# A decoder trunk on one core: inverse root on ScalarE with a Newton step, x for sums on the queue of weights, sum steps tied to value tiles

## The chip, the core and the metric

The kernel runs on one core of one Trainium2 chip. A core has five engines with queues of their own: PE (TensorE, the matrix unit), DVE (VectorE), ACT (ScalarE), POOL (GpSimd) and SP (SyncE, here only an issuer of transfers). Each works through its own instructions in order and waits for the others by semaphores. The metric is the device time of one execution in microseconds (us); before the change three runs took 1052.62, 1054.11 and 1057.05, a median of 1054.11.

## The reference

One layer of a decoder trunk on 512 tokens of width 1024, all in fp32. One projection of x gives queries, keys and values for three attentions and three gates; the branches are projected, gated, summed and projected again; a layer norm follows, then a squared-ReLU MLP with a gated embedding, and a second norm. What the change touches is in these lines:

```python
# differential attention: two softmax maps, and an RMS norm of each head's output
w = prob[:, :, 0] - lam * prob[:, :, 1]
o = o * lax.rsqrt(jnp.mean(jnp.square(o), axis=-1, keepdims=True) + RMS_EPS) * norm_g

# dilated attention, (window, dilation) = (128,1), (512,4), (2048,16); heads of one slot
# are combined by the softmax of their log-denominators
wts = jax.nn.softmax(jnp.stack(lses, axis=0), axis=0)
o = wts[0][..., None] * outs[0] + wts[1][..., None] * outs[1] + wts[2][..., None] * outs[2]

m = mixer(x, ...)
x = layer_norm(DEEPNORM_ALPHA * x + m, ln1_g, ln1_b)
hid = jax.nn.relu(x @ w_up)
c = jnp.square(hid) @ w_down
x = layer_norm(DEEPNORM_ALPHA * x + c + sigmoid(x @ w_ple_gate) * (p @ w_ple), ln2_g, ln2_b)
```

## The kernel before, in words

**Products in two parts.** Every weight chunk of 128x1024 fp32 is loaded into a buffer `raw` (L182, on SP's queue), cast on ACT to a high part `wh` (L212), and the rest `wl = raw - wh` is taken on DVE (L214). The other operand is split likewise, and one product is three matmuls: high by high, low by high, high by low (L87 to L89, and the same three in L420 to L422, L453 to L455, L648 to L650 and others). `raw` is a ring of seven buffers, `wh` and `wl` rings of six, so a load, a cast and a subtraction each wait for the ring's oldest buffer.

**Seven products in place of eight.** Larger products are computed in a scheme of seven block products, which needs sums of blocks. Sums of weights are made in DRAM by transfers that add: `sum_steps` (L958) issues them on POOL's queue, each an adding one (L985) or a plain copy (L987), into `vsum`, `msum`, `gsum`, `usum` and `dsum`; later they are loaded like any other weight. Each sum step depends by hand (the line after L987) on `lows[0]`, the fourth to last L214 issued, which spreads the steps over the main stream. How many are issued after each work item is told by a credit: an item adds its size times its rate (2.5 by default, 1.4 for items of value tiles, 0.5 for those of the sevenfold value scheme), and 0.56 late in the kernel.

**Sums of x for the value product** of the dilated heads are made on DVE. `value_forms` (L343) loads the eight blocks of x^T into `xr` (L347, 256 KB each), forms the sums `fr` (L363, L370, L388) and splits them into `u7`, `u6`, `u4`, `u5` (L237 on ACT, L238 on DVE), which are stored in `vf`. `value_pair` (L395) multiplies them (L420 to L422) and combines the results into the value tiles `dl_v` (L427 to L441). `load_xr` (L324) loads x a second time, for the sums of the mixer's gates (L331). Both sets are issued on POOL's queue, tied to the last L214 (`lows[-1]`).

**The main stream and the heads beside it.** The items (one item is the matmuls into one PSUM bank and its evacuation) stand in a list. Between two items `step` (L1814) advances the attention heads that are active: each head is a generator, and a `yield` is a place at which it lets the main stream go on. So where a `yield` stands decides how many products lie on PE between two steps of a head, and, since each engine is in order, what lies in front of each instruction.

**A dilated head** (`dil_head`, L1661): scores on PE (L1677, L1693), bias and maximum on DVE (L1680, L1701), negated maxima (L1684, L1705), exponentials with row sums on ACT (L1686, L1708), per-row statistics gathered (L1711, L1714) and moved to the other token order by small matmuls (L1718, L1720). Then comes a chain of small DVE operations of 128x8 (L1724 to L1740, with one exponential on ACT, L1735) that gives the combining weights; L1742 and L1746 scale the probabilities by them, L1761 and L1770 transpose these on PE, and L1782, L1787 multiply by the values. In head 0 six extra `yield`s stand ahead of L1761.

**A block of differential attention** (`da_block`, L1589): scores (L131, L132), softmax on DVE and ACT (L1600 to L1614), transposes (L1620), product with the values (L1634), squares with their sum on ACT (L1638). The root of the norm is taken of four values per token, `ss`, in a tile of 128x4: L1643 scales and adds on DVE, L1644 raises to the power -1/2 on POOL, L1645 multiplies by the softmax denominators on DVE. L101 on DVE, in another function, writes the low parts of the queries and keys (`da_klb` among them), whose next user is in the chain of products L648.

**Value tiles** that are not made by the sevenfold scheme (`v_items`, L445) are copied out of PSUM by `cp`, which alternates between ACT and DVE.

Of the kernel before, what the change touches and what calls it, by code (L numbers as in the profile page):

```python
# [13 lines left out]
AF = mybir.ActivationFunctionType  # L14
OP = mybir.AluOpType
# [3 lines left out]
P = 128  # L19
# [36 lines left out]
def trunk(tc, a, out):  # L56
    nc = tc.nc
    es = ExitStack()
    with es:
# [17 lines left out]
        def small(name, n):  # L77
            return one.tile([P, n], F32, name=nm(name), tag=f"sm{n}", bufs=12 if n < 8 else 8)
# [14 lines left out]
        def cp(o, i):  # L93
            flip[0] ^= 1
            if flip[0]:
                nc.scalar.copy(o, i)
            else:
                nc.vector.tensor_copy(o, i)
# [37 lines left out]
        ORDERED, AHEAD = 17, 4  # L136
        loads, chunks, placed = [], [], []
        lows = deque(maxlen=4)
        st = {"dma": 0, "split": 0}

        def load(src, w, own=False):
# [56 lines left out]
        def split_next():  # L198
            c = chunks[st["split"]]
            w, off = c["w"], c.get("off", 0)  # L200
            if c.get("pre"):
                c["pre"]()
            if c.get("dst") is None:
                h = ring.tile([P, 1024], F32R, name=nm("wh"), tag="wh", bufs=RING)
                lo = ring.tile([P, 1024], F32R, name=nm("wl"), tag="wl", bufs=RING)
                parts = [(h[:, :w], lo[:, :w], 0, w)]
                c["h"], c["l"] = parts[0][:2]
            else:
                parts = c["dst"]
            for h, lo, a0, a1 in parts:  # L210
                raw = c["from"]["raw"][:, off + a0:off + a1]
                i = nc.scalar.copy(h, raw)  # L212
                st["cast"] = getattr(i, "ins", i)
                i = nc.vector.tensor_sub(lo, raw, h.bitcast(F32))  # L214
                st["low"] = getattr(i, "ins", i)
                lows.append(st["low"])
            for t in (c["from"], *c.get("also", ())):
                t["uses"] -= 1
            st["split"] += 1
# [10 lines left out]
        items = []  # L230
# [14 lines left out]
        xt = a["xT"]  # L245
# [78 lines left out]
        def load_xr():  # L324

            r = {}
            for h in range(2):
                for th in range(2):
                    for kp in range(2):
                        t = slot("xr")  # L330
                        i = nc.gpsimd.dma_start(t.rearrange("p (k t) -> p k t", k=2),  # L331
                                                xt[:, 4 * h + 2 * kp:4 * h + 2 * kp + 2, 256 * th:256 * th + 256])
                        tc.add_manual_dep(getattr(i, "ins", i), lows[-1].name, mybir.DependencyInfo(
                            mybir.DependencyClass.Sync, mybir.DependencyReason.DATA), reason="not ahead of time")
                        r[h, th, kp] = t
            return [[r[h, th, kp] for kp in range(2)] for h in range(2) for th in range(2)]
# [6 lines left out]
        def value_forms():  # L343

            xr = [slot("xr") for _ in range(8)]
            for k, t in enumerate(xr):
                i = nc.gpsimd.dma_start(t, xt[:, k, :])  # L347
                tc.add_manual_dep(getattr(i, "ins", i), lows[-1].name, mybir.DependencyInfo(
                    mybir.DependencyClass.Sync, mybir.DependencyReason.DATA), reason="not ahead of time")

            def blk(kh, k, th):
                return xr[4 * kh + k].rearrange("p (t c) -> p c t", c=4)[:, 2 * th:2 * th + 2, :]

            def new():
                ts = [slot("fr") for _ in range(2)]
                return ts, [ts[k // 2].rearrange("p (k c t) -> p k c t", k=2, c=2)[:, k % 2] for k in range(4)]

            def parts(p, ts):
                form(vf, p, ts)
                vf[p] = [[(h[:, r * P:r * P + P], lo[:, r * P:r * P + P]) for r in range(2)] for h, lo in vf[p]]  # L360

            def neg_sub(o, i, j):
                nc.vector.scalar_tensor_tensor(o, i, -1.0, j, op0=OP.mult, op1=OP.subtract)  # L363

            for _ in range(WAIT):
                yield
            f7, o7 = new()
            with tc.issue_after(st["low"]):
                for k in range(4):
                    nc.vector.tensor_sub(o7[k], blk(1, k, 1), blk(0, k, 1))  # L370
            parts(7, f7)
            yield
            f6, o6 = new()
            with tc.issue_after(st["low"]):
                for k in range(4):
                    neg_sub(o6[k], o7[k], blk(0, k, 0))
            yield
            parts(6, f6)
            yield
            f4, o4 = new()  # L380
            for k in range(4):
                neg_sub(o4[k], o6[k], blk(1, k, 0))
            yield
            parts(4, f4)
            yield
            f1, o1 = new()
            for k in range(4):
                nc.vector.tensor_sub(o1[k], blk(0, k, 0), blk(0, k, 1))  # L388
            yield
            parts(5, f1)  # L390
            yield
# [53 lines left out]
        def v_items(nv, name, g):  # L445
            cs = [chunk(a["wv"][nv, c].rearrange("p k n -> p (k n)"), 1024) for c in range(4)]
            for tt in range(4):
                def mm(ps, tt=tt):
                    for k in range(8):
                        c = cs[k // 2]  # L450
                        s = slice((k % 2) * 512, (k % 2) * 512 + 512)
                        x1, x2 = xh[k][:, tt * P:tt * P + P], xl[k][:, tt * P:tt * P + P]
                        nc.tensor.matmul(ps, x1, c["h"][:, s], start=k == 0, stop=False)  # L453
                        nc.tensor.matmul(ps, x1, c["l"][:, s], start=False, stop=False)  # L454
                        nc.tensor.matmul(ps, x2, c["h"][:, s], start=False, stop=k == 7)  # L455
                        if k == 3:
                            yield

                def ev(ps, tt=tt):
                    if name == "sb_v":  # L460
                        v = [slot(name, F32R).rearrange("p (h two d) -> p h two d", two=2, d=64) for _ in range(2)]
                        pv = ps.rearrange("p (h d) -> p h d", d=64)
                        for i in range(2):
                            hs = slice(4 * i, 4 * i + 4)
                            nc.scalar.copy(v[i][:, :, 0, :], pv[:, hs, :])
                            nc.vector.tensor_sub(v[i][:, :, 1, :], pv[:, hs, :], v[i][:, :, 0, :].bitcast(F32))
                        V[name, g, tt] = v
                    else:
                        t = slot(name)
                        cp(t, ps)  # L470
                        V[name, g, tt] = t
                item(cs if tt == 3 else [], mm, ev, need=cs)
                items[-1]["rate"] = 1.4

        nt, nv = 2, 0
        order = main_order()
# [18 lines left out]
        last_exp = [None]  # L495
# [187 lines left out]
            item([], mm, ev, size=0.08)  # L683

        last_plain = len(items)
        for it in items:
            it.setdefault("rate", 2.5)
        def first_gate(tt, half):
            g = gate_sig(1, tt, half)
            nc.vector.tensor_mul(merged[tt, half], merged[tt, half], g)  # L690
# [267 lines left out]
        def sum_steps():  # L958
# [24 lines left out]
            def issue(o, i, plus):  # L983
                if plus:
                    i = nc.gpsimd.dma_start(o, i, accum_op=OP.add, max_dma_last_dim=4096)  # L985
                else:
                    i = nc.gpsimd.dma_start(o, i, max_dma_last_dim=4096)  # L987

                tc.add_manual_dep(getattr(i, "ins", i), lows[0].name, mybir.DependencyInfo(
                    mybir.DependencyClass.Sync, mybir.DependencyReason.DATA), reason="spread over the main stream")  # L990

            w = a["wv"].rearrange("g c p k n -> g c p (k n)")
# [596 lines left out]
        def da_block(hd, qb):  # L1589
# [50 lines left out]
            if da_left[hd] == 0:  # L1640
                yield

                nc.vector.tensor_scalar(ss, ss, 1.0 / P, EPS, op0=OP.mult, op1=OP.add)  # L1643
                nc.gpsimd.tensor_tensor(ss, ss, mhalf.to_broadcast([P, 4]), OP.pow)  # L1644
                nc.vector.tensor_mul(ss, ss, da_rr[hd])  # L1645
                yield
                on = slot("on")
                nc.vector.tensor_mul(on.rearrange("p (b d) -> p b d", b=4), po.rearrange("p (b d) -> p b d", b=4),
                                     ss.unsqueeze(2).to_broadcast([P, 4, P]))
# [11 lines left out]
        def dil_head(hd):  # L1661
            while any(("dl_q", 4 * g + hd) not in T or ("dl_k", 4 * g + hd) not in T for g in range(3)):
                yield

            while hd == 1 and ("dl_v", 1, 3) not in V:
                yield
            q = [T["dl_q", 4 * g + hd] for g in range(3)]
            k = [T["dl_k", 4 * g + hd] for g in range(3)]
# [77 lines left out]
                nc.vector.tensor_scalar(o, o, mxx[:, c:c + 1], None, op0=OP.mult)  # L1746
            yield

            for _ in range(6 if hd == 0 else 0):
                yield  # L1750

            src0 = {}
# [89 lines left out]
        for n, it in enumerate(items):  # L1842
# [36 lines left out]
            if 12 <= n < wout_at + 12:  # L1879
                credit += it["size"] * it.get("rate", 1.0)  # L1880
            elif n > ple_at + 6:
                credit += 0.56
            while credit >= 1:
                credit -= 1
                next(sum_steps_, None)
# [139 lines left out]
```

## Time and profile before

| what | us |
|---|---|
| three runs, median (lowest to highest) | 1054.11 (1052.62 to 1057.05) |
| the profiled execution, its own time | 1053.95 |
| its span in the trace | 1052.0 |
| PE busy | 1037.5 |
| DVE busy | 763.5 |
| ACT busy | 582.9 |
| POOL busy | 177.7 |

The span goes from the first to the last instruction of the profiled execution; its own time holds some 2 us more around it. Busy times are sums over the instructions of an engine. A row of the waits names an engine and line, what released it, and then the total, the number and the longest of these waits in us. A row of the windows gives a stretch, its length, the busy time of PE, its weight loads (PEld), DVE, ACT and POOL with instructions in brackets, the granted clock, the share of the transfer engines, and GB/s. A row of the timeline gives start, length, engine, line, operation, result and source, shapes, and in square brackets the idle time ahead of it with what ended it. A row of a line gives the shortest, median and longest duration in ns, then the first and last start in us.

### The profile page before, as it was taken

To read this page: it belongs to the slowest core of one execution; us is meant where nothing else is said; L and a number is where in the kernel's file an instruction comes from. 1 tells how busy PE (TensorE), PEld (TensorE's weight loads), DVE (VectorE), ACT (ScalarE), POOL (GpSimd) and SP (SyncE) were. 2 spreads that over 40 slices of the span, in tenths; PEclk is the share of its full clock that TensorE was granted. 3 is DMA by queue.
4 is the path that set the end of the run, shared out by engine and by line. 5 is a ranking of instruction groups with operands and counts; after the bars stand their busy time and mean duration, and the time that the engine had idled before them with its cause. 6 is when DMAs were issued, how large, how long until landed. Compare 5 with 4: busy or idle time off the path is not lost.

```text
span 1052.0 us, 15035 instructions
## 1 busy us (share of the span) xinstructions
PE 1037.5 (99%) x5474; PEld 883.7 (84%) x5474; DVE 763.5 (73%) x1356; ACT 582.9 (55%) x990; POOL 177.7 (17%) x271
## 2 busy tenths in 40 slices
PE   9999999999999999999999999999999999999997
PEld 6887788888888887888888888888999889889885
DVE  6888667749864746788666664888778877877966
ACT  6666545526444645667554723675666665566651
POOL 0012401320203322211121240111121111111000
PEclk9999999999999999999999999999999999999998
DMA  8348965995847999547998996269999899998512
GB/s 320 112 162 256 216 199 195 312 277 186 275 115 220 305 283 271 182 173 238 280 340 269 309 333 198 87 208 324 332 327 320 285 289 295 313 277 281 190 35 80
DMA packets 72761, 254.32 MB, mean 242 GB/s; under 512 B 8968, under 2 KB 9880, under 8 KB 72688
## 3 DMA queue, kind: packets, MB, share of 16 engines
q0 software_dynamic: 32464, 116.21, 42.2%
q1 hardware_dynamic: 39648, 136.24, 35.6%
q8 instruction: 43, 0.70, 0.3%
q10 hardware_dynamic: 576, 0.92, 0.2%
q14 instruction: 30, 0.25, 0.1%
HBM read 251.21 MB, written 106.98 MB: 340 GB/s over the span
## 4 chain that ended last, share of the span: by engine, by line
PE 84%; DMA 9%; DVE 3%; ACT 2%; issue 1%; POOL 0%; SPq 0%; DVEq 0%; POOLq 0%; ACTq 0%
PE mm L87 8%; PE mm L89 7%; PE mm L88 7%; PE at L1147 4%; PE at L1148 4%; PE at L1149 4%; DMA msum<-in_wgm_dram 4%; PE at L556 3%; PE at L555 3%; PE at L554 3%; PE mm L453 2%; PE mm L455 2%; PE mm L454 2%; DMA gsum<-gsum 2%; PE at L89 1%; PE at L88 1%
## 5 line engine op out<-in xcount | busy, mean ns | idle before, releaser
L214 DVE TENSOR_TENSOR wl<-raw,wh 128x1024 fp32r<-128x1024 f32 x251 | 305.3, 1222 | 126.6 <-ACT wh L212 124.4
L212 ACT CAST wh<-raw 128x1024 fp32r<-128x1024 f32 x251 | 262.7, 1050 | 234.0 <-PE mm L88 127.1
L87 PE MATMUL mm<-xhT,wh 128*128 128x512 f32 x304 | 121.1, 398 | 0.0
L89 PE MATMUL mm<-xhT,wl 128*128 128x512 f32 x304 | 119.0, 391 | 0.0
L88 PE MATMUL mm<-xlT,wh 128*128 128x512 f32 x304 | 118.8, 391 | 0.0
L1147 PE MATMUL at<-wh,hh 128*128 128x512 f32 x188 | 73.7, 392 | 0.0
L1148 PE MATMUL at<-wl,hh 128*128 128x512 f32 x188 | 73.7, 392 | 0.0
L87 PE MATMUL mm<-x1hT,wh 128*128 128x256 f32 x256 | 73.6, 288 | 0.0
L1149 PE MATMUL at<-wh,hl 128*128 128x512 f32 x188 | 73.1, 389 | 0.0
L88 PE MATMUL mm<-x1lT,wh 128*128 128x256 f32 x256 | 72.3, 283 | 0.0
L89 PE MATMUL mm<-x1hT,wl 128*128 128x256 f32 x256 | 71.8, 283 | 0.0
L89 PEld LDWEIGHTS mm<-xhT,wl 128*128 128x128 f32 x304 | 57.1, 188 | 12.3
L87 PEld LDWEIGHTS mm<-xhT,wh 128*128 128x128 f32 x304 | 57.2, 188 | 11.6 <-issue 0.4
L88 PEld LDWEIGHTS mm<-xlT,wh 128*128 128x128 f32 x304 | 57.2, 188 | 10.4
L87 PEld LDWEIGHTS mm<-x1hT,wh 128*128 128x128 f32 x256 | 48.8, 191 | 4.7 <-ACT up L1081 2.8
L88 PEld LDWEIGHTS mm<-x1lT,wh 128*128 128x128 f32 x256 | 48.8, 191 | 1.5
L89 PEld LDWEIGHTS mm<-x1hT,wl 128*128 128x128 f32 x256 | 48.6, 191 | 0.0
L985 POOL DMA_DIRECT2D usum<-in_wu_dram x32 | 27.6, 879 | 107.6 <-DVE wl L214 75.7
L1149 PEld LDWEIGHTS at<-wh,hl 128*128 128x128 f32 x188 | 35.3, 188 | 7.7
L1147 PEld LDWEIGHTS at<-wh,hh 128*128 128x128 f32 x188 | 35.5, 189 | 6.0
L1148 PEld LDWEIGHTS at<-wl,hh 128*128 128x128 f32 x188 | 35.5, 189 | 5.5
L985 POOL DMA_DIRECT2D dsum<-in_wd_dram x28 | 23.5, 848 | 96.5 <-DVE wl L214 74.7
(563 smaller groups left out, 2662.3 us busy)
## 6 DMA issues: line engine op xcount, KB each, us to landing
usum<-in_wu_dram POOLq DMA_DIRECT2D x48, 512.0 KB, 9.7
dsum<-in_wd_dram POOLq DMA_DIRECT2D x42, 512.0 KB, 9.0
raw<-in_wt_dram SPq DMA_DIRECT2D x38, 512.0 KB, 6.5
msum<-in_wgm_dram POOLq DMA_DIRECT2D x36, 512.0 KB, 12.7
raw<-usum SPq DMA_DIRECT2D x32, 512.0 KB, 8.1
raw<-dsum SPq DMA_DIRECT2D x28, 512.0 KB, 7.3
raw<-in_wd_dram SPq DMA_DIRECT2D x25, 512.0 KB, 5.3
raw<-msum SPq DMA_DIRECT2D x24, 512.0 KB, 6.0
```

The costliest lines, as they stand in the source:

```text
L87: nc.tensor.matmul(ps, wh, xh, start=start, stop=False, skip_group_check=True)
L88: nc.tensor.matmul(ps, wh, xl, start=False, stop=False, skip_group_check=True)
L89: nc.tensor.matmul(ps, wl, xh, start=False, stop=stop, skip_group_check=True)
L212: i = nc.scalar.copy(h, raw)
L214: i = nc.vector.tensor_sub(lo, raw, h.bitcast(F32))
L554: nc.tensor.matmul(ps, h[:, q], c["h"][:, n], start=go, stop=False, skip_group_check=True)
L555: nc.tensor.matmul(ps, h[:, q], c["l"][:, n], start=False, stop=False, skip_group_check=True)
L556: nc.tensor.matmul(ps, lo[:, q], c["h"][:, n], start=False, stop=end, skip_group_check=True)
L985: i = nc.gpsimd.dma_start(o, i, accum_op=OP.add, max_dma_last_dim=4096)
L1147: nc.tensor.matmul(ps, h[:, q], c["h"][:, s], start=go, stop=False, skip_group_check=True)
L1148: nc.tensor.matmul(ps, h[:, q], c["l"][:, s], start=False, stop=False, skip_group_check=True)
L1149: nc.tensor.matmul(ps, lo[:, q], c["h"][:, s], start=False, stop=end, skip_group_check=True)
```

## The change

Five things are changed.

1. The power on POOL (L1644) is replaced by a logarithm and an exponential on ACT, y = exp(-0.5 ln(ss)), and one Newton step on DVE, y(1.5 - 0.5 ss y y), in three operations of 128x4. The head's `yield` now stands between ACT's part and DVE's. `last_exp` has the table of the sigmoid loaded behind the last of these exponentials.
2. The loads of x for sums (both `value_forms` and `load_xr`) are issued on SP's queue.
3. The copies of value tiles in `v_items` are all on DVE.
4. A second list `marks` of four entries holds each L214 once and each of these copies twice, and the sum steps depend on `marks[0]` in place of `lows[0]`. Rates: value items 2.5 (1.4 before), other items 2.5 for the first 45 and 1.5 behind them (2.5 for all before), and late in the kernel 0.6 (0.56 before).
5. Dilated head 0 begins only when the last sum of x (`vf[5]`) exists, and its extra `yield`s ahead of L1761 are two (six before).

```diff
@@ -136,6 +136,7 @@
         ORDERED, AHEAD = 17, 4
         loads, chunks, placed = [], [], []
         lows = deque(maxlen=4)
+        marks = deque(maxlen=4)
         st = {"dma": 0, "split": 0}
 
         def load(src, w, own=False):
@@ -214,6 +215,7 @@
                 i = nc.vector.tensor_sub(lo, raw, h.bitcast(F32))
                 st["low"] = getattr(i, "ins", i)
                 lows.append(st["low"])
+                marks.append(st["low"])
             for t in (c["from"], *c.get("also", ())):
                 t["uses"] -= 1
             st["split"] += 1
@@ -328,7 +330,7 @@
                 for th in range(2):
                     for kp in range(2):
                         t = slot("xr")
-                        i = nc.gpsimd.dma_start(t.rearrange("p (k t) -> p k t", k=2),
+                        i = nc.sync.dma_start(t.rearrange("p (k t) -> p k t", k=2),
                                                 xt[:, 4 * h + 2 * kp:4 * h + 2 * kp + 2, 256 * th:256 * th + 256])
                         tc.add_manual_dep(getattr(i, "ins", i), lows[-1].name, mybir.DependencyInfo(
                             mybir.DependencyClass.Sync, mybir.DependencyReason.DATA), reason="not ahead of time")
@@ -344,7 +346,7 @@
 
             xr = [slot("xr") for _ in range(8)]
             for k, t in enumerate(xr):
-                i = nc.gpsimd.dma_start(t, xt[:, k, :])
+                i = nc.sync.dma_start(t, xt[:, k, :])
                 tc.add_manual_dep(getattr(i, "ins", i), lows[-1].name, mybir.DependencyInfo(
                     mybir.DependencyClass.Sync, mybir.DependencyReason.DATA), reason="not ahead of time")
 
@@ -467,10 +469,12 @@
                         V[name, g, tt] = v
                     else:
                         t = slot(name)
-                        cp(t, ps)
+                        i = nc.vector.tensor_copy(t, ps)
+                        marks.append(getattr(i, "ins", i))
+                        marks.append(getattr(i, "ins", i))
                         V[name, g, tt] = t
                 item(cs if tt == 3 else [], mm, ev, need=cs)
-                items[-1]["rate"] = 1.4
+                items[-1]["rate"] = 2.5
 
         nt, nv = 2, 0
         order = main_order()
@@ -683,8 +687,8 @@
             item([], mm, ev, size=0.08)
 
         last_plain = len(items)
-        for it in items:
-            it.setdefault("rate", 2.5)
+        for j, it in enumerate(items):
+            it.setdefault("rate", 2.5 if j < 45 else 1.5)
         def first_gate(tt, half):
             g = gate_sig(1, tt, half)
             nc.vector.tensor_mul(merged[tt, half], merged[tt, half], g)
@@ -986,7 +990,7 @@
                 else:
                     i = nc.gpsimd.dma_start(o, i, max_dma_last_dim=4096)
 
-                tc.add_manual_dep(getattr(i, "ins", i), lows[0].name, mybir.DependencyInfo(
+                tc.add_manual_dep(getattr(i, "ins", i), marks[0].name, mybir.DependencyInfo(
                     mybir.DependencyClass.Sync, mybir.DependencyReason.DATA), reason="spread over the main stream")
 
             w = a["wv"].rearrange("g c p k n -> g c p (k n)")
@@ -1641,9 +1645,15 @@
                 yield
 
                 nc.vector.tensor_scalar(ss, ss, 1.0 / P, EPS, op0=OP.mult, op1=OP.add)
-                nc.gpsimd.tensor_tensor(ss, ss, mhalf.to_broadcast([P, 4]), OP.pow)
+                y = small("ir", 4)
+                nc.scalar.activation(y, ss, AF.Ln)
+                e = nc.scalar.activation(y, y, AF.Exp, scale=-0.5)
+                last_exp[0] = getattr(e, "ins", e)
+                yield
+                nc.vector.scalar_tensor_tensor(ss, ss, -0.5, y, op0=OP.mult, op1=OP.mult)
+                nc.vector.tensor_mul(ss, ss, y)
+                nc.vector.scalar_tensor_tensor(ss, ss, 1.5, y, op0=OP.add, op1=OP.mult)
                 nc.vector.tensor_mul(ss, ss, da_rr[hd])
-                yield
                 on = slot("on")
                 nc.vector.tensor_mul(on.rearrange("p (b d) -> p b d", b=4), po.rearrange("p (b d) -> p b d", b=4),
                                      ss.unsqueeze(2).to_broadcast([P, 4, P]))
@@ -1663,6 +1673,8 @@
                 yield
 
             while hd == 1 and ("dl_v", 1, 3) not in V:
+                yield
+            while hd == 0 and 5 not in vf:
                 yield
             q = [T["dl_q", 4 * g + hd] for g in range(3)]
             k = [T["dl_k", 4 * g + hd] for g in range(3)]
@@ -1746,7 +1758,7 @@
                 nc.vector.tensor_scalar(o, o, mxx[:, c:c + 1], None, op0=OP.mult)
             yield
 
-            for _ in range(6 if hd == 0 else 0):
+            for _ in range(2 if hd == 0 else 0):
                 yield
 
             src0 = {}
@@ -1879,7 +1891,7 @@
             if 12 <= n < wout_at + 12:
                 credit += it["size"] * it.get("rate", 1.0)
             elif n > ple_at + 6:
-                credit += 0.56
+                credit += 0.6
             while credit >= 1:
                 credit -= 1
                 next(sum_steps_, None)
```

## The prediction

> **What bounds the kernel now.** I read the page first, then the waits of TensorE, then a table of windows.
>
> ```profile
> span 1052.0 us, 15035 instructions
> PE 1037.5 (99%) x5474; PEld 883.7 (84%) x5474; DVE 763.5 (73%) x1356; ACT 582.9 (55%) x990; POOL 177.7 (17%) x271
> ...
> PE mm L648 <- DVE da_klb L101: 1.1, 1, 1.1
> PE at L1720 <- DVE r L1714: 1.0, 1, 1.0
> PE at L131 <- ACT da_ka L122: 0.8, 2, 0.6
> PE at L1718 <- DVE r L1711: 0.6, 1, 0.6
> PE mm L420 <- ACT dl_v L427: 0.5, 1, 0.5
> PE at L131 <- ACT da_kb L124: 0.3, 1, 0.3
> PE mm L420 <- ACT dl_q L285: 0.2, 1, 0.2
> ...
> 240.00:260.00 20.00, 18.85 (x90) 17.07 (x89) 18.52 (x55) 13.09 (x29) 0.74 (x2) 1.00 0.46 156
> 260.00:280.00 20.00, 20.00 (x96) 16.79 (x95) 19.04 (x36) 11.12 (x16) 3.05 (x6) 1.00 0.82 281
> 400.00:420.00 20.00, 18.27 (x96) 14.72 (x94) 14.23 (x51) 9.74 (x22) 5.22 (x7) 1.00 1.03 284
> ```
>
> PE is busy 99% of the span, so the change can win only what PE waits: the seven waits (two more, of the first 8 us, are not touched) add up to 4.5 us. In the windows (length, then busy time of PE, PEld, DVE, ACT, POOL) PE loses time where VectorE is full (18.5 and 19.0 of 20 us at 240 to 280) and around 400 to 420. An idle stretch costs a little more than its length:
>
> ```profile
> 249.14 0.40 PE L422 MATMUL mm<-wh,xlT 128*128 128x512 f32 x1
> 250.08 0.51 PE L420 MATMUL mm<-wh,u7h 128*128 128x512 f32 x1 [0.55 <-ACT dl_v L427]
> 251.19 0.41 PE L1718 MATMUL at<-r,fold 128*128 128x32 f32 x2 [0.60 <-DVE r L1711]
> ```
>
> Products otherwise start 0.23 us apart. Here the starts are 0.94 and 1.11 apart, so idle times of 0.55 and 0.60 cost 0.71 and 0.88: a factor of 1.4. All seven waits are then worth 4.5 x 1.4 = 6.3 us, 0.6% of the time, and that is the most that the change can win.
>
> **Part 1: x on the queue of weights, and its gain.**
>
> ```profile
> 233.19 0.61 DVE L370 TENSOR_TENSOR fr<-xr,xr 128x256 f32<-128x256 f32 x1 [6.16 <-DMA xr<-in_xT_dram]
> ...
> 214.26 1.67 POOL L347 DMA_DIRECT2D xr<-in_xT_dram  x3 [5.12 <-DVE wl L214]
> 229.11 0.54 POOL L347 DMA_DIRECT2D xr<-in_xT_dram  x1 [3.07 <-PE at L1571]
> ```
>
> The eight x loads of L347 stand on POOL's queue among the sum steps, and the last is issued at 229.1. VectorE stands 6.2 us before the first form (L370), and the forms then collide with the first dilated head: hence the full windows and the waits of L1718 and of both L420. On SP the same loads wait only for their buffers. By the rows around them I lay their issue at 214 to 222 and their landing before 230, so the forms begin near 228. That removes 0.2 + 0.5 + 0.6 = 1.3 us of idle time. What is queued behind them on SP are weights:
>
> ```profile
> SPq L182 <- DVE wl L214: 709.8, 204, 34.9
> L212 ACT CAST wh<-raw 128x1024 fp32r<-128x1024 f32 x251 | 262.7, 1050 | 234.0 <-PE mm L88 127.1
> ```
>
> SP waits for ring buffers to come free (709.8 us in all), and the cast waits for PE, not for a landing: weights are early. The 8 us that eight loads hold SP's queue are covered by the weights that lie ready in the ring of raw and split buffers; with that cover gone PE would lose up to those 8 us. I cost it at 0. The second set of x loads (L331) is treated alike.
>
> **Part 2: the root on ScalarE.**
>
> ```profile
> DVE ms L1645 <- POOL ms L1644: 7.3, 4, 4.0
> 400.76 1.05 POOL L1644 TENSOR_TENSOR ms<-ms,mhalf 128x4 f32<-128x4 f32 x1
> ```
>
> The power of L1644 takes 1.05 us on POOL, but VectorE waited 7.3 us for four of them, 4.0 in one case, because POOL stood in a sum step until 400.8. After it come L1711, L1701, L1708 and L1714, and L1714 is the wait of 1.0 before L1720. Two ACT operations and three more VectorE operations on 128x4 replace it; the nearest rows are ACT L1735 and L1736 below, 0.22 and 0.17 us. Chain of the new root: 2 x 0.22 + 3 x 0.17 = 0.95, against 4.0. So L1714 comes some 1.2 us earlier or more (its own ScalarE work sits in between), which takes away the 1.0. The same head's later order also puts L101 of da_klb ahead of small work of the next head, and its wait of 1.1 at L648 goes, with only 0.2 us to spare by my laying-out. The 0.8 and 0.3 of L131 stay. The added 8 ACT and 12 VectorE operations (4 x 0.95 us in all) lie beside PE.
>
> Gain of parts 1 and 2: 1.3 + 1.0 + 1.1 = 3.4 us idle, x 1.4 = **4.8 us**. Bounds: 0 (nothing arrives earlier) and 6.3.
>
> **Part 3: the first dilated head.** It now waits for the last form (vf[5]) and leaves out four of six extra yields. In the order of instructions of the changed program this puts the two L1720 matmuls, then only two products, then the transposes L1761, on PE. Before:
>
> ```profile
> 255.38 0.34 PE L1720 MATMUL at<-r,foldT 128*128 128x32 f32 x2
> 265.54 0.71 PE L1761 MATMUL at<-ident,L 128*128 128x128 f32 x5
> ...
> 310.63 0.30 PE L1720 MATMUL at<-r,foldT 128*128 128x32 f32 x2
> 310.98 0.23 DVE L1724 TENSOR_TENSOR sel<-at,pick 128x64 f32<-128x64 f32 x1 [0.87 <-PE at L1720]
> 312.07 0.22 ACT L1735 ACTIVATE ex<-ex 128x16 f32<-128x16 f32 x1 [2.19 <-DVE ex L1734]
> 312.32 0.17 DVE L1736 TENSOR_TENSOR mxx<-ex,st 128x8 f32<-128x8 f32 x1 [0.28 <-ACT ex L1735]
> 313.23 0.81 DVE L1742 TENSOR_SCALAR L<-L,mxx 128x128 f32<-128x128 f32 x3
> ```
>
> Between 255.4 and 265.5 PE had 10 us of products, while VectorE did L1724 to L1742, on which L1761 rests. The chain costs least in a head where VectorE had nothing else: from the start of L1720 at 310.63 to the end of the first L1742 (313.23, and 0.3 for one of the three), 2.9 us. In the changed order VectorE has four more instructions inside this chain: two L214 and one each of L434 and L435.
>
> ```profile
> L214 DVE TENSOR_TENSOR wl<-raw,wh 128x1024 fp32r<-128x1024 f32 x251 | 305.3, 1222 | 126.6 <-ACT wh L212 124.4
> L434 DVE TENSOR_TENSOR dl_v<-dl_v,mm x1: 680/680/680, 267.3 to 267.3; 128x512 f32<-128x512 f32 x1
> L435 DVE TENSOR_TENSOR dl_v<-dl_v,dl_v x2: 684/684/684, 269.0 to 271.9; 128x512 f32<-128x512 f32 x2
> ```
>
> Chain: 2.9 + 2 x 1.22 + 0.68 + 0.68 = 6.7, less 0.3 that one of them hides of ScalarE's turn, less 0.2 for overlap: 6.2. PE's cover is L1720 and two products, 0.14 + 2 x 0.23 = 0.6. **Loss 5.6 us.** Bounds: 2.9 - 0.6 = 2.3 if nothing else stood in the chain; and the 8.2 us that the chain took before among other work (255.38 to the first start of L1742 in its row, 263.5) less 0.6 = 7.5.
>
> ```profile
> L1742 DVE TENSOR_SCALAR L<-L,mxx x16: 276/347/351, 263.5 to 414.9; 128x256 f32<-128x256 f32 x12, 128x128 f32<-128x128 f32 x4
> ```
>
> Further up in the same head all of L1680 and L1701 now follow the last form in one piece, while L427's copy of the next value tile queues on ScalarE behind casts of 1.05, and L1711 behind one more L214 of 1.22. Laid end to end, PE waits about 1.0 us at an L420 for that copy and 1.0 at L1718. Bounds of each: 0, and one cast and one L214 together, 2.3. I take 1.0, between them, as in both places the laid-out PE is only one such instruction ahead. **Loss 2.0 us.**
>
> **The clock after a long stall.**
>
> ```profile
> 1044.00:1045.00 1.00, 0.17 (x2) 0.00 (x0) 1.00 (x4) 0.00 (x0) 0.00 (x0) 1.00 0.98 367
> 1046.00:1046.50 0.50, 0.00 (x0) 0.00 (x0) 0.50 (x3) 0.00 (x0) 0.00 (x0) 0.94 0.00 0
> 1046.50:1047.00 0.50, 0.00 (x0) 0.00 (x0) 0.50 (x1) 0.00 (x0) 0.00 (x0) 0.50 0.00 0
> L1325 PE MATMUL at<-zero x9: 609/634/634, 1.3 to 4.6; 128*128 128x512 bf16 x9
> ```
>
> In the tail PE stops at 1044.2 and its granted clock falls to 0.5 near 1046.4, 2.3 us later. A stall of 5.6 us is longer than that. At the head, after idleness, nine matmuls of 512 columns start over 3.3 us, 0.41 apart in place of 0.23. The same slow start behind the stall would lose 3.3 x (1 - 0.23/0.41) = 1.4 us; bounds 0 and 1.4, and I take 0.8, as it is not shown that such a start follows a stall in mid-kernel. **Loss 0.8 us.** [...]
>
> **Part 4: where the sum steps hang.**
>
> ```profile
> POOL msum L985 <- DVE wl L214: 35.4, 3, 28.2
> POOL msum L987 <- DVE wl L214: 49.3, 5, 31.0
> msum<-in_wgm_dram POOLq DMA_DIRECT2D x36, 512.0 KB, 12.7
> ```
>
> Sum steps now hang on value tiles too (each counted twice), and rates of 2.5, 1.5 and 0.6 move them: those of 200 to 320 us by some 40 to 60 earlier, those of the last stage by up to 70 later. The least distance from a late step to the load that reads its sum becomes 21.5 us by the instruction order laid on the old times, against a landing of 12.7. I cost it at 0; the long idle stretches of POOL (28.2 and 31.0) should go. All eight value copies on VectorE add four of 0.68 there, beside PE.
>
> **Sum**, on the profiled execution (1053.95 us, of which the span is 1052.0): 1053.95 + 5.6 + 2.0 + 0.8 - 4.8 = 1057.55. That execution is 0.16 under the median of the runs, 1054.11; I forecast **1057.6**.
>
> **Rivals.**
> 1. *The chain is short after all*: stall 2.3, no others, the gains as above: 2.3 - 4.8 = -2.5, **1051.5**; with every wait gone and no stall -6.3, 1047.8. For it: VectorE saves 6.2 us early. Against: the chain begins with a PE result, so no earlier start shortens it. It decides if the two L214 are finished before L1720.
> 2. *VectorE stays the bound of 240 to 275*, the slower side: 7.5 at L1761, 2.3 twice, 1.4 of clock, with only part 2's gain of (1.0 + 1.1) x 1.4 = 2.9: +10.6, **1064.7**. For it: 18.5 and 19.0 of 20 us busy. It decides if the forms end after PE has reached L1718.
> 3. *A sum comes late*: a POOL wait of 31.0 before a step whose lead is 21.5 holds PE 9.5 us: 1057.6 + 9.5 = **1067**. Against: the waits become shorter.
> 4. *The change does not do what it says*: x waits on SP for the same buffers as long as on POOL, and the root is held on ScalarE behind casts, so only the wait of L648 goes (1.1 x 1.4 = 1.5), with all the losses: 1053.95 + 8.4 - 1.5 = **1060.9**. For it: x takes over buffers that PE frees. Against: laid on the old times, all but the last of those buffers are free by 215.
>
> **How the numbers follow.** Forecast 0.58 (own range 1054 to 1061), rival 1 0.16, rival 2 0.14, rival 3 0.05, rival 4 0.07. A measurement of this kernel tells about 0.5%, 5.3 us, from no change: bounds of 1048.8 and 1059.4. Faster: 0.06, the best part of rival 1. Slower: rivals 2, 3 and 4 and a quarter of the forecast, 0.41. Within: 0.53. The range leaves out rival 3 and the ends of rivals 1 and 2, some 0.16: 1050 to 1064.5.
>
> **What would show it.** The idle time before L370 gone (part 1); L1645 waiting for no POOL, and L1720 and L648 gone from PE's waits (part 2); a new line of PE's L1761 waiting for L1742 with 5 us and more near 268 to 274, and L1718 near 1 (part 3); a granted clock under 1.00 behind it; POOL's waits of 28.2 and 31.0 gone (part 4). A PE busy 20 of 20 at 260 to 280 would make the forecast wrong.

## The result and the profile after

| | us |
|---|---|
| changed kernel, median of 5 runs (lowest to highest) | 1068.28 (1067.45 to 1069.03) |
| kernel before, median of 5 runs on the same chip | 1053.51 (1052.62 to 1057.05) |
| ratio, with its 95% interval | 1.0134 (1.0116 to 1.0152) |
| span of the profiled execution, before and after | 1052.0 and 1066.7 |

The changed kernel is 1.3% slower, 14.7 us by the two spans. Its line numbers have moved: the x loads L347 are L349 now, the first forms L370 are L372, L285 is L287, the products L420 to L422 are L422 to L424, L427 is L429, L1718 is L1730, L1742 is L1754 and the transposes L1761 are L1773. First the waits of TensorE after the change (total, number and longest in us):

```profile
PE mm L422 <- ACT dl_q L287: 8.6, 1, 8.6
PE at L1773 <- DVE L L1754: 4.9, 1, 4.9
PE at L1730 <- DVE r L1723: 1.1, 1, 1.1
PE at L131 <- ACT da_ka L122: 0.8, 2, 0.6
PE mm L422 <- ACT dl_v L429: 0.4, 1, 0.4
PE at L131 <- ACT da_kb L124: 0.3, 1, 0.3
```

The waits of L1720 and L648 are gone. Three of the new ones have a place in the forecast (4.9, 1.1 and 0.4), and the largest, 8.6, has none. The windows show the same (length, busy time of PE, PEld, DVE, ACT, POOL, granted clock, share of the transfer engines, GB/s):

```profile
220.00:240.00 20.00, 16.65 (x78) 13.56 (x76) 7.50 (x12) 3.73 (x6) 0.83 (x1) 0.98 1.04 309
240.00:260.00 20.00, 14.72 (x62) 13.59 (x63) 12.14 (x17) 7.16 (x10) 0.81 (x1) 0.76 0.55 166
280.00:300.00 20.00, 16.63 (x73) 14.84 (x74) 13.42 (x28) 6.06 (x8) 4.08 (x7) 0.91 0.61 174
400.00:420.00 20.00, 20.00 (x110) 17.33 (x109) 8.63 (x37) 6.62 (x22) 3.49 (x5) 1.00 0.69 190
```

PE works all of 400 to 420, where it had lost 1.7 us. It loses 8.6 between 220 and 260 with VectorE nearly idle (7.5 of 20 us, the opposite of what the window of 240 to 260 had shown before), and the clock is low behind. Where the 8.6 us come from is read from the engines one after another. ScalarE, timeline:

```profile
237.68 0.62 ACT L239 CAST u7h<-fr 128x512 fp32r<-128x512 f32 x1 [8.57 <-DVE fr L372]
243.05 0.62 ACT L239 CAST u7h<-fr 128x512 fp32r<-128x512 f32 x1 [4.75 <-DVE fr L372]
244.63 0.60 ACT L287 ACTIVATE dl_q<-mm 128x512 f32<-128x512 f32 x1
```

The copy that frees PE's bank (`dl_q`, L287) stands on ScalarE behind two casts of the first forms, and these wait for VectorE. VectorE, timeline:

```profile
234.47 0.61 DVE L372 TENSOR_TENSOR fr<-xr,xr 128x256 f32<-128x256 f32 x1 [7.89 <-DMA xr<-in_xT_dram]
237.04 0.61 DVE L372 TENSOR_TENSOR fr<-xr,xr 128x256 f32<-128x256 f32 x1 [1.96 <-DMA xr<-in_xT_dram]
239.23 0.61 DVE L372 TENSOR_TENSOR fr<-xr,xr 128x256 f32<-128x256 f32 x1 [0.87 <-DMA xr<-in_xT_dram]
242.41 0.60 DVE L372 TENSOR_TENSOR fr<-xr,xr 128x256 f32<-128x256 f32 x1 [2.57 <-DMA xr<-in_xT_dram]
```

Each form waits for one more load of x, of 256 KB, and the forms start 2.2 to 3.2 us apart. The last form of the four starts at 242.4; before the change the last two ran from 235.4. Yet the loads were not issued late (SP, then POOL beside it):

```profile
213.92 7.65 SPq L349 DMA_DIRECT2D xr<-in_xT_dram  x8
...
207.04 0.81 POOL L989 DMA_DIRECT2D msum<-in_wgm_dram  x1 [3.88 <-DVE wl L215]
207.59 0.79 POOL L991 DMA_DIRECT2D msum<-msum  x1
210.93 0.54 POOL L991 DMA_DIRECT2D msum<-msum  x1 [2.55 <-DMA msum<-in_wgm_dram]
214.95 0.52 POOL L991 DMA_DIRECT2D msum<-msum  x1 [3.48 <-DMA msum<-in_wgm_dram]
217.38 0.52 POOL L991 DMA_DIRECT2D msum<-msum  x1 [1.92 <-DMA msum<-in_wgm_dram]
```

All eight were issued between 213.9 and 221.6, up to 8 us earlier than on POOL. It is their way that became longer. The time from issue to landing of this line, before (first row) and after (second), each from the view of its line:

```profile
DMA to landing us min/median/max: 6.0/14.4/15.4
```

```profile
DMA to landing us min/median/max: 10.5/17.8/22.4
```

And the slow clock, after, where the two long stalls end:

```profile
239.00:239.50 0.50, 0.00 (x0) 0.00 (x0) 0.27 (x1) 0.00 (x0) 0.00 (x0) 0.66 0.99 246
249.40:249.80 0.40, 0.40 (x3) 0.40 (x2) 0.09 (x1) 0.28 (x1) 0.00 (x0) 1.00 0.00 0
283.00:283.50 0.50, 0.13 (x1) 0.14 (x1) 0.50 (x3) 0.00 (x0) 0.00 (x0) 1.00 0.69 197
283.50:284.00 0.50, 0.50 (x3) 0.46 (x3) 0.50 (x3) 0.00 (x0) 0.00 (x0) 0.53 0.74 229
286.90:287.40 0.50, 0.50 (x3) 0.38 (x3) 0.00 (x0) 0.00 (x0) 0.00 (x0) 0.95 0.00 0
```

```profile
246.75 0.63 PE L422 MATMUL mm<-wh,xhT 128*128 128x512 f32 x1
247.18 0.63 PE L423 MATMUL mm<-wl,xhT 128*128 128x512 f32 x1
250.07 0.40 PE L422 MATMUL at<-wh,xhT 128*128 128x512 f32 x1
250.31 0.39 PE L423 MATMUL at<-wl,xhT 128*128 128x512 f32 x1
```

Nine products behind the first stall start 0.43 us apart in place of 0.24, some 1.8 us; behind the second, seven transposes take 0.2 in place of 0.1 each and four products 0.43, some 1.5. By the busy times of the two profiles PE's idle time (span less busy time) rose from 14.5 to 25.9 us, and its busy time, which holds the slow products, from 1037.5 to 1040.8. So the 14.7 us are 11.4 of waits and 3.3 of slow clock.

### The profile page after: what moved, and what is told of

It reads as the page before. It is cut to its first block, busy times and chain, and to the rows that moved or that the text cites. A ratio compares the mean times of both kernels' runs of the same rounds, so it can differ in the third digit from the quotient of the medians.

```text
span 1066.7 us, 15045 instructions
## 1 busy us (share of the span) xinstructions
PE 1040.8 (98%) x5474; PEld 886.3 (83%) x5474; DVE 768.8 (72%) x1372; ACT 582.6 (55%) x994; POOL 161.9 (15%) x251
## 4 chain that ended last, share of the span: by engine, by line
PE 90%; DVE 4%; DMA 2%; ACT 2%; issue 2%; POOL 0%; DVEq 0%; POOLq 0%
PE mm L87 10%; PE mm L89 9%; PE mm L88 9%; PE at L1151 4%; PE at L1152 4%; PE at L1153 4%; PE at L558 3%; PE at L559 3%; PE at L560 3%; PE mm L455 2%; PE mm L457 2%; PE mm L456 2%; DMA xr<-in_xT_dram 2%; PE at L89 1%; PE at L88 1%
## 5 line engine op out<-in xcount | busy, mean ns | idle before, releaser
L213 ACT CAST wh<-raw 128x1024 fp32r<-128x1024 f32 x251 | 262.9, 1050 | 239.3 <-PE mm L88 127.2
L88 PEld LDWEIGHTS mm<-xlT,wh 128*128 128x128 f32 x304 | 57.2, 188 | 10.5
L989 POOL DMA_DIRECT2D msum<-in_wgm_dram x24 | 21.2, 923 | 126.7 <-DVE wl L215 62.8
## 6 DMA issues: line engine op xcount, KB each, us to landing
msum<-in_wgm_dram POOLq DMA_DIRECT2D x36, 512.0 KB, 10.5
```

Source lines behind the costliest of these rows:

```text
L88: nc.tensor.matmul(ps, wh, xl, start=False, stop=False, skip_group_check=True)
```

## The experiments

### Which part makes x late

The texts put on record ahead of the first runs weigh two theories. By A, sum transfers that are already under way hold the transfer engines when x is asked for, whichever queue x uses. By B, it is SP's queue that makes x late, as its eight loads get only a share beside POOL's sums.

The kernel before with x on SP alone (two lines: `nc.gpsimd.dma_start` to `nc.sync.dma_start` in `value_forms` and `load_xr`).

> The kernel before with only the two sets of x loads moved to SP's queue. Theory A: fewer sums are in flight when x is asked for, so the last x lands at or before 235, PE loses no more than before: 1051 to 1054. Theory B: x shares the engines with POOL's sums as in the changed kernel, lands near 242, and PE waits about 8 us more and runs slow behind it: 1062 to 1065. No wait ahead of the transposes of head 0 in either, as 43 products lie between.

Measured 1059.67 us, ratio 1.0058 (1.0036 to 1.008). TensorE's wait, VectorE's first form and POOL's timeline:

```profile
PE mm L420 <- ACT dl_q L285: 5.2, 1, 5.2
```

```profile
237.99 0.61 DVE L370 TENSOR_TENSOR fr<-xr,xr 128x256 f32<-128x256 f32 x1 [11.10 <-DMA xr<-in_xT_dram]
```

```profile
207.35 1.64 POOL L985 DMA_DIRECT2D msum<-in_wgm_dram  x2 [3.60 <-DVE wl L214]
214.11 2.47 POOL L985 DMA_DIRECT2D msum<-in_wgm_dram  x3 [5.12 <-DVE wl L214]
```

Theory A is out in its plain form: moving x alone costs 6 us. But the POOL rows show more than B does. In the kernel before, three sum steps stood behind the last x load in POOL's queue:

```profile
229.64 2.62 POOL L985 DMA_DIRECT2D msum<-in_wgm_dram  x3
```

With x gone from that queue three are issued at 214.1, 15 us earlier, and run beside x.

The changed kernel with x back on POOL (the reverse of those two lines).

> The changed kernel with both sets of x loads back on POOL's queue, all else as changed. Theory A (transfers already issued for sums hold the DMA engines when x is asked for; which queue x uses matters little): x then stands behind the same sums on POOL, the last x lands at 236 to 241 in place of 242.3, and PE still waits 3 to 8 us at the evacuation of dl_q; time 1063 to 1068. Theory B (the SP queue is what makes x late, as its eight loads get one share beside POOL's): the last x lands near 235 as before the change, the wait of 8.6 us and its slow clock go, time 1057 to 1059. In both the wait of 4.9 us ahead of the transposes of head 0 stays.

Measured 1067.77 us, ratio 1.014 (1.012 to 1.0161): as slow as the changed kernel. PE waits 6.1 us at the evacuation of `dl_q`, and the first form:

```profile
238.43 1.19 DVE L372 TENSOR_TENSOR fr<-xr,xr 128x256 f32<-128x256 f32 x2 [10.88 <-DMA xr<-in_xT_dram]
```

So B is out too: x is late on either queue. Here it is late by its issue, not by its way: to landing it takes 10.4 us at the median, less than the 14.4 of the kernel before, but POOL waits 10.7 us for sum transfers ahead of x loads (4.7 before), and the last is issued at 235.7 in place of 229.1:

```profile
235.68 0.54 POOL L349 DMA_DIRECT2D xr<-in_xT_dram  x1 [1.04 <-DMA msum<-msum]
```

The changed kernel with the sum steps hung and paced as before:

```diff
-                tc.add_manual_dep(getattr(i, "ins", i), marks[0].name, mybir.DependencyInfo(
+                tc.add_manual_dep(getattr(i, "ins", i), lows[0].name, mybir.DependencyInfo(
...
-                items[-1]["rate"] = 2.5
+                items[-1]["rate"] = 1.4
...
-            it.setdefault("rate", 2.5 if j < 45 else 1.5)
+            it.setdefault("rate", 2.5)
...
-                credit += 0.6
+                credit += 0.56
```

> The changed kernel with the sum steps hung and paced as before (tied to the fourth to last split, rates 1.4, 2.5 and 0.56); value copies stay on VectorE, x on SP, root on ScalarE, head 0 as changed. Theory A: the sums in flight at 214 us are fewer, the last x lands by 235, the wait of 8.6 us falls under 2 us: 1056 to 1060. Theory B: x is as late as in the changed kernel, the wait stays at 7 us or more: 1066 to 1069.

Measured 1066.23 us, ratio 1.0124 (1.0104 to 1.0144), wait at `dl_q` 6.7 us. By its number this is near B, but with the two runs above it says that either part is enough to make x late, so that undoing one wins back only 2 us.

Theory C, formed from these: what counts is how much sum traffic is in flight, or is let go, while x is under way. To test it in the kernel before, x goes to SP and the sums step aside: from the x loads in `value_forms` to the last of the first four forms no sum step is handed out, and each later one depends on that form.

```diff
+        held = {"on": False, "dep": None}
...
+            held["on"] = True
             for _ in range(WAIT):
...
-                    nc.vector.tensor_sub(o7[k], blk(1, k, 1), blk(0, k, 1))
+                    i = nc.vector.tensor_sub(o7[k], blk(1, k, 1), blk(0, k, 1))
+            held.update(on=False, dep=getattr(i, "ins", i))
...
+                if held["dep"] is not None:
+                    tc.add_manual_dep(getattr(i, "ins", i), held["dep"].name, mybir.DependencyInfo(
+                        mybir.DependencyClass.Sync, mybir.DependencyReason.DATA), reason="behind x for sums")
...
-            while credit >= 1:
+            while credit >= 1 and not held["on"]:
```

> The kernel before with x on SP's queue, and with the sum steps that come up between the issue of x and its last first form held back until that form is made (eight steps of 512 KB). Theory C, from the four runs so far: x was late in all of them because sums were in flight or issued beside it; on POOL the x loads also kept the later sums behind them, on SP they do not. Then x lands within some 5 to 9 us of its issue, the last by 230, PE does not wait at the evacuation of dl_q, and the waits of 0.5 and 0.6 us of the kernel before shrink too: 1051 to 1053. Theory B (the SP queue itself makes x late): the last x lands at 238 or later and PE waits 5 us: 1058 to 1061.

Measured 1051.22 us, ratio 0.9989 (0.9979 to 0.9999). Issue to landing of the eight x loads in the run with x on SP alone, then in this one, and its sum steps on POOL:

```profile
DMA to landing us min/median/max: 10.9/18.6/22.4
```

```profile
DMA to landing us min/median/max: 4.3/6.4/6.9
```

```profile
231.50 6.68 POOL L988 DMA_DIRECT2D msum<-in_wgm_dram  x8 [35.77 <-DVE fr L372]
```

The same loads on the same queue take 6.4 us in place of 18.6 at the median when eight sum steps stand still, and neither the wait at `dl_q` nor those of L427 and L1718 are left. Theory C holds: 6 us slower has become 0.1% faster by that alone. A wait of 1.4 us at L1720 stays, as this kernel has the root on POOL. What SP's queue adds once the sums are held is not shown, as no run holds them with x on POOL.

### Head 0

Three runs take its two edits apart. The first is the changed kernel with both undone:

```diff
-            while hd == 0 and 5 not in vf:
-                yield
...
-            for _ in range(2 if hd == 0 else 0):
+            for _ in range(6 if hd == 0 else 0):
```

> The changed kernel without the wait of head 0 for the last sum of x and with its six extra yields: 43 products between the statistics matmuls and the transposes in place of 2. Theory (both A and B): the waits of 4.9 us at the transposes and of 1.1 us ahead of the statistics, and the slow clock behind them (1.4 us), go: 7 us less, 1061 to 1062. Rival C: as x is late, the head's work then collides with the forms and PE waits elsewhere for what was saved: 1065 or more.

Measured 1058.95 us, ratio 1.0053 (1.0036 to 1.0069). The stalls at the transposes and ahead of the statistics are gone, and 9.3 us with them, 2 more than expected: the wait at `dl_q` is 6.8 in place of 8.6 us. Rival C of that text is out.

The second is the kernel before with these two edits alone (the same lines added).

> The kernel before with only head 0's new place: it waits for the last sum of x and has two extra yields, which leaves two products between the statistics matmuls and the transposes. x is on POOL as before and lands by 236. Theory: PE waits 4.9 us ahead of the transposes and about 1 us ahead of the statistics, and its clock falls behind the longer stall (1.4 us), against the 1.3 us of small waits that go: 1059 to 1061. Rival: with x early the chain on VectorE meets less other work, and the stall is 3 us or less: 1055 to 1057.

Measured 1062.74 us, ratio 1.0104 (1.0087 to 1.0122), a little more than expected. TensorE's waits:

```profile
PE at L1763 <- DVE L L1744: 5.1, 2, 4.9
PE at L1720 <- DVE r L1713: 1.1, 1, 1.1
PE mm L420 <- ACT dl_q L285: 0.9, 1, 0.9
```

L1763 are the transposes here. Their stall is 4.9 us in this kernel, where x is early, and 4.9 in the changed kernel, where x is late: it rests on the order alone.

The third is the changed kernel with six yields in place of two and its wait kept (one line).

> The changed kernel with six extra yields in head 0 in place of two, its wait for the last sum of x kept: 38 products lie between the statistics matmuls and the transposes in place of two. Theory: the two yields alone make the stall of 4.9 us and the slow clock behind it; both go, the late x stays: 1060 to 1062. Rival: the late begin of the head makes it, and 3 us or more of wait remain there: 1065 or more.

Measured 1062.53 us, ratio 1.01 (1.008 to 1.012). TensorE's waits have no line of the transposes, while the wait ahead of the statistics stays:

```profile
PE mm L422 <- ACT dl_q L287: 7.9, 1, 7.9
PE at L1730 <- DVE r L1723: 1.1, 1, 1.1
```

So the two yields make the stall of 4.9, and the late begin makes the 1.1.

### The root

The kernel before with only the lines of the root changed.

> The kernel before with only the root on ScalarE (logarithm, exponential and the Newton step for the power). Theory: L1645 no longer waits for POOL, the wait of 1.0 us at L1720 (1.2 with its restart) goes; whether the 1.1 at L648 goes is open, as the run with x back on POOL still had it. 1051 to 1053. Rival: the root was hidden but for that one head and the saving is under what the runs resolve: 1053 to 1054, but the profile then still lacks the wait at L1720.

Measured 1052.01 us, ratio 0.9987 (0.9975 to 0.9999). TensorE's waits no longer have L1720, and still have:

```profile
PE mm L648 <- DVE da_klb L101: 1.1, 1, 1.1
```

VectorE waits for no power any more (7.3 us for the four of them before). The wait at L648 is not the root's: it stays here and with x on POOL in the changed kernel, and is missing in every run that has x on SP. What in the move of the x loads takes it away was not followed.

### All together

The changed kernel with the sums held, as above but from two items earlier (in the driver, `if n == v_from[0] - 2: held["on"] = True`).

> The changed kernel with nothing else than the sum steps held back from shortly before the issue of x until its first forms are made (as in the run with x on SP and sums held); head 0 stays as changed. This sets up what the prediction had assumed, x landed before 230. Theory C: the wait of 8.6 us and its slow clock (1.8 us) go, and what stays is the forecast's own sum: about 5 us at the transposes, 1 to 2 us of L1718 and L427's waits as they were named before the change, 1.4 us of slow clock, less the 4.8 us of waits won: 1056 to 1059. Rival D: the held sums come late or crowd the engines behind, or VectorE is full again, and 1062 or more remains.

Measured 1059.15 us, ratio 1.0062 (1.0049 to 1.0075). The first forms no longer wait for x, and PE's waits at `dl_q`, L1720 and L648 are gone. The form, then the largest waits that are left behind the first 8 us (L1779 are the transposes, L1736 the first statistics product):

```profile
228.18 1.14 DVE L374 TENSOR_TENSOR fr<-xr,xr 128x256 f32<-128x256 f32 x2 [1.10 <-PE at L1581]
```

```profile
PE at L1779 <- DVE L L1760: 5.0, 1, 5.0
PE at L1736 <- DVE r L1729: 1.1, 1, 1.1
PE mm L425 <- ACT dl_v L432: 0.4, 1, 0.4
```

The time is just above the range expected. Theory C's sum is right to within some 2 us: with x there in time, 9.1 us of the changed kernel's 14.8 are gone, where 10.4 were expected, and the largest waits that remain are head 0's.

The same with head 0 as before.

> The same with head 0 as before as well (no wait for the last sum of x, six extra yields): of the changed kernel remain the root on ScalarE, x on SP, all value copies on VectorE, and the sum steps tied to them with their rates. Theory C: neither stall is left, and the waits of 240 to 252 and of L1720 are gone: 1048 to 1051, faster than the kernel before by 0.3 to 0.5%. Rival D: 1053 or more, as the held sums crowd what follows.

Measured 1052.22 us, ratio 0.9991 (0.9982 to 1.0001): not the 1048 to 1051 of theory C, and not the 1053 of rival D either. What is left is of the kind that rival D names, in TensorE's waits and VectorE's timeline of this run (L1777 are the transposes of another head):

```profile
PE at L1777 <- DVE L L1758: 1.4, 1, 1.4
```

```profile
296.87 0.43 DVE L1400 COPY shf<-sh 128x512 f32<-128x512 f32 x1 [0.93 <-DMA sh<-rv]
298.13 0.43 DVE L1400 COPY shf<-sh 128x512 f32<-128x512 f32 x1 [0.83 <-DMA sh<-rv]
```

Bias tables (`sh`), which are loaded on POOL's queue, come late, VectorE stands for them ahead of the chain of that head, and PE waits for that chain. What makes them late stays open. That the held sums are let go at once is not enough: the next run lets its held sums go at once too, and there VectorE makes three copies of this kind in one piece, from 294.20 to 295.29, and waits for no transfer ahead of them.

The kernel before with the root on ScalarE, x on SP and the sums held, and nothing else of the change.

> The kernel before with the root on ScalarE, x on SP and the sum steps held until the first forms, without the tie to value tiles, the rates, the copies and head 0's new place. The two alone were worth 0.1% each, and with x on SP alone the wait ahead of the statistics of the head at 403 us was 1.4 us, which the root takes away. Theory: 1049 to 1051. Rival: the waits only move on, 1051 to 1053.

Measured 1049.21 us, ratio 0.9968 (0.9956 to 0.9981): faster than both kernels. The 1.4 us that the text gives to x on SP alone belong to the run that also holds the sums; with x on SP alone that wait was 0.7. TensorE's largest wait behind the first 8 us:

```profile
PE at L131 <- ACT da_ka L122: 0.9, 2, 0.7
```

Little is left to win from waits. The root, x on SP and the held sums are worth 0.3% together. The run above adds the tie to value tiles, the rates, the copies on VectorE and the earlier hold, and is 3.0 us slower; these four were not taken apart.

## Why the prediction was wrong

**The step that failed** is part 1. It laid the issue of x at 214 to 222, which was right (213.9 to 221.6), and "their landing before 230", and costed what moves on the queues at 0. Landing took 10.5 to 22.4 us, and VectorE's idle time ahead of the first forms, which was to go, grew from 6.4 to 13.3 us. A row of the kernel before already had 14.4 us at the median for these very loads, and the window in which they were under way shows why:

```profile
215.00:225.00 10.00, 10.00 (x49) 8.40 (x48) 4.35 (x8) 3.41 (x6) 2.54 (x5) 1.00 1.05 249
```

The engines were full (a share of 1.05), so an issue by 222 and a landing 8 us later was no sound sum. Two things were missed:

- POOL's queue was also an order. There the x loads kept three sum steps behind them; when they left, these came forward by 15 us (229.6 before, 214.1 with x on SP alone) and ran beside them. I counted what stands behind x on SP, and not what had stood behind it on POOL and was now free.
- Part 4 noted that the sums of 200 to 320 move forward by 40 to 60 us, and looked for late sums only. That earlier traffic fills the engines at the very time at which x is under way was not asked. Either of the two is enough to bring x some 5 us later (`dl_q` wait of 5.2 to 6.7 us); both together make that wait 8.6, or 6.8 with head 0 as before.

What hung on x was also missed: the copy of `dl_q` on ScalarE, in order behind the casts of the forms. The prediction knew that wait as 0.2 us, a line among seven, and did not ask what it would be if x came 7 us later; rival 4 has x waiting no less than before, but not more.

How much of the transfer engines x would get was not asked either. In the changed kernel the four forms, each waiting for one more load of 256 KB, start 2.2 to 3.2 us apart, so x gets an estimated 80 to 120 GB/s, while the window of 220 to 240 shows 309 in all. So on SP's queue x had a share here, an estimated 0.26 to 0.39 of what was moved, and not a place at the front.

**What was right.** Head 0: 5.6 us were forecast at the transposes, 4.9 to 5.0 measured, in every kernel with two products there; the order of instructions gave it and nothing else moved it, and VectorE's timeline has in the chain just the four further instructions that were named. The waits ahead: 1.0 at L1718 was 1.1; 1.0 at L427's copy was 0.4. The clock: 0.8 was taken with a bound of 1.4, and behind this stall about 1.5 were lost. The root: L1720's wait went. L648's went as well, but for another reason than the one given: the move of x, not the root, takes it away. POOL's waits of 28.2 and 31.0 us ahead of `msum` steps are gone, as part 4 had said; the longest at the same lines are 20.8 and 12.3.

With x early, as assumed, the changed kernel is 6.0 us slower than the kernel before on the same chip, against 3.5 in the forecast and 14.8 measured for the whole change. So of an error of 11.3 us late x is 8.7. The 2.5 that are left hide two errors that partly cancel, by the profiles of the two kernels. PE's idle time rose by 3.1 us, where 4.2 were forecast (5.6 + 2.0 - 3.4), so the waits were laid out rather long. Its busy time rose by 2.3, where the forecast has a fall of 0.6: 0.8 for the clock, less the 1.4 that the factor adds to the gains. The slow clock explains a part of this; the rest stays open.

**Range and rivals.** 1068.28 lies outside 1050 to 1064.5. Rival 2 (1064.7) had the right side by the wrong mechanism: VectorE was to be full from 240 to 275, and it stood mostly idle up to 242 (busy 7.5 of 20 us from 220 to 240, and not at all from 240 to 242). Rival 3 came nearest, with 1067, but by luck: it looked at late sums, and the sums were early. No rival had late x.

## What to carry to other kernels

Before a transfer is moved to another queue, look at what stood behind it on the old one: that work is set free. Here, with x on SP alone and the transfer engines full (a share of 1.05 from 220 to 240), x took 18.6 us to landing at the median in place of 14.4. What brought the load forward that others wait for was holding bulk traffic back while it was under way, not the other queue alone: 18.6 us became 6.4. And where a chain of small operations stands between two instructions of one engine, count the products that lie between them: 43, 38 and 2 were the difference between no stall and 4.9 us.

## What the hardware showed beside that

In the changed kernel the granted clock of TensorE changed at other times than those at which the stalls began and ended. PE stopped at 236.7 and the clock fell to 0.50 near 239.2, 2.5 us later; it stopped at 278.5 and the clock fell near 283.5, 5 us later and after PE had started again at 283.4. It came back near 249.4 and 286.9, 10.2 and 3.4 us behind the fall. What sets these times was not shown. Behind the stall of 4.9 us some 1.5 us more were lost, although the clock was still full when it ended (1.00 from 283.0 to 283.5).
